# Down projection of a hybrid decoder layer: three of four chunks leave PSUM through ScalarE and reach the residual by accumulating DMAs

## The chip, the cores and the metric

One core of one Trainium2 chip runs the whole program in one launch. The metric is the device time of that core in microseconds (us). Three runs of the kernel before gave a median of 2453.39 us (2452.91 to 2453.67).

## The reference

One layer of a decoder trunk works on 1024 prompt positions and 8 sample positions, which the kernel keeps side by side as 1032 columns. The layer has a recurrent part (two linear recurrences, merged and projected by `w_out`) and then the part that matters here:

```
x  = x + g1 * (u @ w_out)
h2 = rmsnorm(x, norm_mlp) * (1 + sc2) + sh2
x  = x + g2 * (square(relu(h2 @ w_up)) @ w_down)
y  = rmsnorm(x, norm_final)
```

The width is 1024 and the hidden width of the last block is 4096. `g2` is one number for each of the 1024 channels: the same for all prompt positions, another for each of the 8 sample positions. All data are float32.

## The kernel before, in words

Activations are stored transposed: a plane is a tile of 128 channels (the partitions) by `NT` = 1032 columns, so x is eight planes `x1[0]` to `x1[7]`. For float32 accuracy every matmul operand is split into a high part and a remainder, and each product is three matmuls (high by remainder, remainder by high, high by high; lines 89 and 1344). A weight block of 128 by 1024 is loaded by SyncE's queue into a staging tile `wr` (three of them), ScalarE makes the high part `wh` (line 57), VectorE the remainder `wl` (line 58). An activation plane is loaded and split in the same way by `load_split_in` (DMA line 925, ScalarE line 926, VectorE line 927).

The up projection produces 32 hidden planes and stores each to DRAM (`ad[j]`) by DMAs from GpSimd's queue (line 1372). The down projection `x1 += g2 * (hidden @ w_down)` is cut into four chunks c = 0 to 3 of the 4096 hidden channels (loop at line 1429). Each chunk takes eight hidden planes as `X` and has eight output planes m. For chunks 0 to 2, `chunk` (line 977) does:

- m = 0, 1, 2 with `dense` (line 120): three column slices of 344, each 24 matmuls into one PSUM tile of tag `acc` (three of them). Beside them VectorE and ScalarE build the operand sums for what follows (`operand_sums`: loads line 968, differences line 1150, split lines 971 and 972).
- m = 3 and 4, then m = 5 and 6, with `strassen_pair` (line 1317): seven block products p in the order 1, 7, 6, 2, 5, 4, 3, each in two column quarters q of 258, each 12 matmuls. Products 6, 5 and 3 go on accumulating in the bank of product 1, and product 4 in that of product 7. Where a partial sum is also part of another result, `keep` (line 1329) copies it to SBUF by ScalarE (products 1, 6, 7); results come out after products 2, 5, 4 and 3.
- The next chunk's eight planes are loaded and split (`following`), and m = 7 is done with `dense`, whose weight split is cut in two parts.

Chunk 3 does m = 0 to 2 with `dense`, and then, after the loop, m = 3 to 7 by column ranges together with the sum of squares of the final norm, and the store of y.

How a result reaches `x1`: after a dense slice `gated_add` (line 1059) runs one VectorE instruction `x = ps * gate + x` (line 1065); for the columns of the last slice, the 8 sample columns take two more (lines 1068 and 1069). After a pair's product 2, 5 or 4, `add_pair` (line 1417) first adds the kept copy to the PSUM tile on VectorE (line 1423, tile `dt`) and then calls `gated_add`; after product 3 it calls `gated_add` alone.

The order of each engine's instructions is fixed when the program is built: the framework orders them by priority and by its own simulated times, and inserts the waits on tiles, buffers and DMAs. Evacuations are issued at a raised priority (lines 92 and 1348). Each engine then works through its list in order.

Tiles that the change takes up: the tags `mt` (2 buffers), `sq` (2), `nrm_y` (2), `nrm_a`, `nrm_t` and `sqa` (1 each) of 128 by 344 float32, which the up projection and `keep` use.

Of the kernel before, what the change touches and what calls it, by code (L numbers as in the profile page):

```python
# [1 line left out]

# [5 lines left out]
F32 = mybir.dt.float32  # L8
# [3 lines left out]
AF = mybir.ActivationFunctionType  # L12
ALU = mybir.AluOpType
# [4 lines left out]
P = 128  # L18
T = 1024
NB = 8  # L20
NT = T + NB
NS = 3
SW = NT // NS
# [16 lines left out]
def cs(s):  # L40
    return slice(s * SW, (s + 1) * SW)
# [6 lines left out]
def load_w(k, src, prio=AHEAD, tiles=None, parts=1):  # L48

    nc = k.nc  # L50
    with k.tc.high_priority(prio):
        wr = stage(k)[:, :KD * P]
        nc.sync.dma_start(wr, src)
        wh, wl = tiles or [k.wp.tile([P, KD * P], F32R, tag=t, name=t, bufs=2) for t in ("wh", "wl")]
        for n in range(parts):
            c = slice(n * KD * P // parts, (n + 1) * KD * P // parts)
            nc.scalar.activation(wh[:, c], wr[:, c], AF.Copy)  # L57
            nc.vector.tensor_tensor(wl[:, c], wr[:, c], wh[:, c].bitcast(F32), op=ALU.subtract)  # L58
    return wh, wl
# [60 lines left out]
def dense(k, src, X, evac, parts=1):  # L120

    w = load_w(k, src, parts=parts)
    return [dense_split(k, w, X, s, evac) for s in range(NS)]
# [935 lines left out]
def gated_add(k, s, dst, base, ps, gate):  # L1059

    nc = k.nc
    c = cs(s) if isinstance(s, int) else s
    w = c.stop - c.start
    n = w if c.stop < NT else w - NB
    nc.vector.scalar_tensor_tensor(dst[:, :n], ps[:, :n], gate[:, 0:1], base[:, :n], ALU.mult, ALU.add)
    if n < w:
        t = k.sp.tile([P, NB], F32, tag="ga", name="ga", bufs=2)
        nc.vector.tensor_tensor(t, ps[:, n:], gate[:, 1:9], op=ALU.mult)
        nc.vector.tensor_tensor(dst[:, n:], t, base[:, n:], op=ALU.add)
# [60 lines left out]
HQ = NT // 4  # L1130
# [186 lines left out]
def strassen_pair(k, srcs, X, evac, last=3):  # L1317


    nc = k.nc  # L1320
    W = strassen_weights(k, srcs)
    bank = {}
    for n in (1, 2, 3):
        for q in range(2):
            tag, bufs = ("rec", 4) if n == 1 else ("acc", 3) if (n, q) != (3, 1) else ("ada", 1)
            bank[n, q] = k.ps.tile([P, 512], F32, tag=tag, name="b%d" % n, bufs=bufs)[:, :HQ]
    snap = {}

    def keep(p, q, acc):
        pool, tag, bufs = {(1, 0): (k.sp, "nrm_y", 2), (1, 1): (k.sp, "nrm_y", 2), (6, 0): (k.sp, "nrm_a", 1),  # L1330
                           (6, 1): (k.sp, "nrm_t", 1), (7, 0): (k.sp2, "sqa", 1), (7, 1): (k.sp2, "s7", 1)}[p, q]
        t = pool.tile([P, HQ if tag == "s7" else SW], F32, tag=tag, name="s%d" % p, bufs=bufs)[:, :HQ]
        k.kept = nc.scalar.activation(t, acc, AF.Copy)
        snap[p, q] = t

    for p in (1, 7, 6, 2, 5, 4, 3) if last == 3 else (1, 7, 6, 5, 4, 3, 2):
        b = {7: 2, 4: 2, 2: 3}.get(p, 1)
        for q in range(2):
            acc = bank[b, q]
            cols = slice(q * HQ, (q + 1) * HQ)  # L1340
            wh, wl = W[p]
            for i, (xh, xl) in enumerate(X[p]):
                sl = slice(i * P, (i + 1) * P)
                for j, (a, x) in enumerate(((wh, xl), (wl, xh), (wh, xh))):
                    nc.tensor.matmul(acc, a[:, sl], x[:, cols], start=(p in (1, 7, 2) and i == 0 and j == 0),  # L1345
                                     stop=(i == KD // 2 - 1 and j == 2), skip_group_check=True)
                tick(k, 3)
            with k.tc.high_priority(AHEAD):
                if p in (1, 6, 7):
                    keep(p, q, acc)  # L1350
                elif p == 2:
                    evac(0, 0, q, snap[1, q], acc)
                elif p == 5:
                    evac(1, 1, q, snap[7, q], acc)
                elif p == 4:
                    evac(1, 0, q, snap[6, q], acc)
                else:
                    evac(0, 1, q, None, acc)


def phase_ffn(k, x1, h2):
    nc = k.nc
    NF = 4 * KD
    up = k.i["w_up"]
    ad = [k.dp.tile([P, NT], F32, name="ad%d" % j) for j in range(NF)]
    bufs = iter(range(1 << 20))

    def out(j, cols):
        n = next(bufs) % 4
        pool, tag = (k.sp2, "mt") if n < 2 else (k.sp, "sq")  # L1370
        r = pool.tile([P, SW], F32, tag=tag, name="r", bufs=2)[:, :cols.stop - cols.start]
        return r, lambda: nc.gpsimd.dma_start(ad[j][:, cols], r)

    def relu2(r, ps):
        nc.scalar.activation(r, ps, AF.Relu)
        nc.vector.tensor_tensor(r, r, r, op=ALU.mult)

    def evac_up(j):
        def f(s, ps):
            r, store = out(j, cs(s))  # L1380
            relu2(r, ps)
            store()
        return f

    ws = [load_w(k, up[j]) for j in range(2)]
    for j, s in [(j, s) for j in range(2) for s in LAST[:2]] + [(0, LAST[2]), (1, LAST[2])]:
        dense_split(k, ws[j], h2, s, evac_up(j))

    T = {n: [] for n in (1, 2, 3, 4)}
    for j in range(2, 6):  # L1390
        dense(k, up[j], h2, evac_up(j))
        strassen_planes(k, h2, T, j - 2)
    X = strassen_operands(h2, T)
    for n in range(6, NF - 2, 2):
        def evac(m, half, q, a, ps, n=n):
            c = half * HN + q * HQ
            r, store = out(n + m, slice(c, c + HQ))
            if a is None:
                relu2(r, ps)
            else:  # L1400
                nc.vector.tensor_tensor(r, a, ps, op=ALU.add)
                nc.vector.scalar_tensor_tensor(r, r, 0.0, r, ALU.max, ALU.mult)
            store()
        strassen_pair(k, (up[n], up[n + 1]), X, evac)

    def add(m):
        return lambda s, ps: gated_add(k, s, x1[m][:, cs(s)], x1[m][:, cs(s)], ps, k.modT[:, 40 + m, :])

    def act(c, j):
        return load_split_in(k, ad[c * KD + j], half_tag("S0" if c % 2 else "S1", j))  # L1410
    down = k.i["w_down"]
    M0 = 3
    aX = []
    for j in range(NF - 2, NF):
        aX += [act(0, i) for i in range(4 * (j - NF + 2), 4 * (j - NF + 3))]
        dense(k, up[j], h2, evac_up(j))
    def add_pair(m0):
        def evac(m, half, q, a, ps):
            c = half * HN + q * HQ
            c = slice(c, c + HQ)  # L1420
            if a is not None:
                t = k.sp.tile([P, SW], F32, tag="sq", name="dt", bufs=2)[:, :HQ]
                nc.vector.tensor_tensor(t, a, ps, op=ALU.add)
                ps = t
            x = x1[m0 + m][:, c]
            gated_add(k, c, x, x, ps, k.modT[:, 40 + m0 + m, :])
        return evac

    for c in range(4):
        ws = [down[c * KD + m] for m in range(KD)]  # L1430
        if c == 3:
            for m in range(M0):
                dense(k, ws[m], aX, add(m))
            break
        aX = chunk(k, ad[c * KD:(c + 1) * KD], aX, ws, add, add_pair, "S1" if c % 2 else "S0",
                   lambda: [act(c + 1, i) for i in range(KD)])
    free = [k.pp.tile([P, NT], F32R, tag=half_tag("S1", i // 2), name="free") for i in range(16)]
    ws = [load_w(k, down[3 * KD + m], tiles=None if m < M0 + 2 else [free[2 * (m - M0) - 4 + n][:, :KD * P] for n in range(2)])
          for m in range(M0, KD)]
    sq, sq2, sums, ra, rs = [t.bitcast(F32) for t in free[11:]]  # L1440
    for m in range(M0):
        sum_sq(k, sums, x1[m], m == 0, (sq, sq2)[m % 2])
    half = iter(range(1 << 20))
    for c in COLS:
        for m in range(M0, KD):
            x = x1[m][:, c]
            dense_split(k, ws[m - M0], aX, c, lambda s, ps: gated_add(k, s, x, x, ps, k.modT[:, 40 + m, :]))
            o = next(half) % 2 * 512
            sum_sq(k, sums[:, c], x, False, sq[:, o:o + c.stop - c.start])
        y = rstd_model(k, sums[:, c], (ra[:, c], rs[:, c], sums[:, c]))  # L1450
        for m in range(KD):
            x = x1[m][:, c]
            nc.vector.scalar_tensor_tensor(x, x, k.norm_final[:, m:m + 1], y, ALU.mult, ALU.mult)  # L1453
            nc.sync.dma_start(k.o["y"][m][:, c], x)
# [181 lines left out]
```

## Time and profile before

| | |
|---|---|
| median of three runs | 2453.39 us |
| the profiled execution | 2456.04 us |
| its span in the profile | 2454.1 us |
| PE, PEld busy | 2419.3, 2355.8 us |
| DVE, ACT, POOL busy | 1736.0, 1155.7, 112.7 us |
| mean DMA rate | 142 GB/s |

PE is TensorE's matmuls, PEld its weight loads, DVE VectorE, ACT ScalarE, POOL GpSimd, SP SyncE; a q behind a name is that engine's sequencer, which also issues DMAs. A group line names the source line, engine, operation, output and inputs with their shapes, then the count, the busy time in us and the mean in ns, then the idle time ahead of it and what ended it. A line of the windows view gives for a stretch of the span the busy time and the count of each engine, the granted clock of TensorE (PEclk, 1 is full), the mean busy share of the 16 DMA engines and what they moved. The view of one source line gives the shortest, the median and the longest duration of its instructions in ns. Matmuls overlap in a pipeline, so the time of one in a group is longer than the distance from one to the next.

### The profile page before, as it was taken

To read this page: it belongs to the slowest core of one execution; us is meant where nothing else is said; L and a number is where in the kernel's file an instruction comes from. 1 tells how busy PE (TensorE), PEld (TensorE's weight loads), DVE (VectorE), ACT (ScalarE), POOL (GpSimd) and SP (SyncE) were. 2 spreads that over 40 slices of the span, in tenths; PEclk is the share of its full clock that TensorE was granted. 3 is DMA by queue.
4 is the path that set the end of the run, shared out by engine and by line. 5 is a ranking of instruction groups with operands and counts; after the bars stand their busy time and mean duration, and the time that the engine had idled before them with its cause. 6 is when DMAs were issued, how large, how long until landed. Compare 5 with 4: busy or idle time off the path is not lost.

```text
span 2454.1 us, 51952 instructions
## 1 busy us (share of the span) xinstructions
PE 2419.3 (99%) x22014; PEld 2355.8 (96%) x22014; DVE 1736.0 (71%) x3019; ACT 1155.7 (47%) x1859; POOL 112.7 (5%) x218
## 2 busy tenths in 40 slices
PE   8999999999999999999999999999999999999998
PEld 7999999999999999999999899999999999999997
DVE  7656666359888888886687757656976666787755
ACT  4544444366555665534566534533533334343331
POOL 0000000000000000001011000000011222000000
PEclk9999999999999999999999999999999999999999
DMA  7333323334544454535445724634233335354231
GB/s 263 123 112 115 117 100 130 116 93 149 175 136 163 135 179 132 169 146 173 140 158 170 267 91 171 233 130 138 92 109 103 113 110 172 124 190 160 74 130 70
DMA packets 113897, 347.86 MB, mean 142 GB/s; under 512 B 20385, under 2 KB 26385, under 8 KB 113649
## 3 DMA queue, kind: packets, MB, share of 16 engines
q1 hardware_dynamic: 96960, 291.68, 35.0%
q0 software_dynamic: 16272, 52.52, 6.2%
q8 instruction: 172, 2.82, 0.5%
q14 instruction: 61, 0.49, 0.1%
q10 hardware_dynamic: 432, 0.35, 0.0%
HBM read 274.91 MB, written 69.85 MB: 140 GB/s over the span
## 4 chain that ended last, share of the span: by engine, by line
PE 49%; DVE 2%; DMA 2%; ACT 1%; issue 1%; SPq 0%; DVEq 0%; POOL 0%; ACTq 0%; POOLq 0%
PE b L1345 26%; PE acc L90 22%; DMA ybc<-rh 1%; DVE wl L58 0%; DMA lo<-yd 0%; DMA lo<-od 0%; ACT wh L57 0%; PE ss L567 0%; PE ss L1087 0%; DVE lo L927 0%; DVE ht L1116 0%; DVE sqa L1080 0%; DMA lo<-ad 0%; DVE x L1453 0%; DVE h2l L1118 0%
## 5 line engine op out<-in xcount | busy, mean ns | idle before, releaser
L90 PE MATMUL acc<-hl,wh 128*128 128x344 f32 x1608 | 527.6, 328 | 0.1
L90 PE MATMUL acc<-hh,wl 128*128 128x344 f32 x1608 | 516.5, 321 | 0.0
L90 PE MATMUL acc<-hh,wh 128*128 128x344 f32 x1608 | 515.6, 321 | 0.0
L1345 PE MATMUL b<-th,wl 128*128 128x258 f32 x1120 | 317.4, 283 | 0.3
L1345 PE MATMUL b<-tl,wh 128*128 128x258 f32 x1120 | 317.3, 283 | 0.0
L1345 PE MATMUL b<-th,wh 128*128 128x258 f32 x1120 | 315.9, 282 | 0.0
L90 PEld LDWEIGHTS acc<-hl,wh 128*128 128x128 f32 x1608 | 302.3, 188 | 5.2 <-issue 2.8
L90 PEld LDWEIGHTS acc<-hh,wh 128*128 128x128 f32 x1608 | 302.5, 188 | 3.9 <-issue 3.9
L90 PEld LDWEIGHTS acc<-hh,wl 128*128 128x128 f32 x1608 | 302.6, 188 | 0.0
L90 PE MATMUL acc<-lo,wh 128*128 128x344 f32 (+3 forms) x792 | 254.0, 322 | 4.1 <-DVE lo L927 2.5
L90 PE MATMUL acc<-hi,wl 128*128 128x344 f32 (+3 forms) x792 | 254.5, 321 | 0.1
L90 PE MATMUL acc<-hi,wh 128*128 128x344 f32 (+3 forms) x792 | 253.5, 320 | 0.0
L1290 DVE TENSOR_TENSOR wl<-wr,wh 128x512 fp32r<-128x512 f32 (+1 forms) x175 | 157.8, 902 | 97.1 <-ACT wh L1308 53.8
L1345 PEld LDWEIGHTS b<-tl,wh 128*128 128x128 f32 x1120 | 211.5, 189 | 4.5 <-issue 4.5
L57 ACT ACTIVATE wh<-wr 128x1024 fp32r<-128x1024 f32 (+1 forms) x140 | 142.8, 1023 | 152.7 <-PE acc L90 75.4
L1345 PEld LDWEIGHTS b<-th,wl 128*128 128x128 f32 x1120 | 211.6, 189 | 2.7 <-DVE wl L1290 2.7
L1345 PEld LDWEIGHTS b<-th,wh 128*128 128x128 f32 x1120 | 211.4, 189 | 0.0
L58 DVE TENSOR_TENSOR wl<-wr,wh 128x1024 fp32r<-128x1024 f32 (+1 forms) x140 | 165.6, 1184 | 64.6 <-ACT wh L57 63.9
L90 PEld LDWEIGHTS acc<-lo,wh 128*128 128x128 f32 x792 | 149.0, 188 | 6.4 <-DVE lo L927 3.3
L90 PEld LDWEIGHTS acc<-hi,wl 128*128 128x128 f32 x792 | 149.4, 189 | 1.9 <-DVE wl L58 1.0
L90 PEld LDWEIGHTS acc<-hi,wh 128*128 128x128 f32 x792 | 149.4, 189 | 0.8
L756 DVE SCALAR_TENSOR_TENSOR cv<-raw,cst,cv 128x1024 f32<-128x1024 f32 x96 | 122.5, 1276 | 0.5
(342 smaller groups left out, 5219.8 us busy)
## 6 DMA issues: line engine op xcount, KB each, us to landing
wr<-w_ssm SPq DMA_DIRECT2D x48, 512.0 KB
wr<-w_ada SPq DMA_DIRECT2D x36, 512.0 KB
lo<-ad SPq DMA_DIRECT2D x32, 516.0 KB
wr<-w_hg SPq DMA_DIRECT2D x32, 512.0 KB
w<-cumd SPq DMA_DIRECT2D x32, 512.0 KB
wr<-w_up SPq DMA_DIRECT2D x32, 512.0 KB
wr<-w_down SPq DMA_DIRECT2D x32, 512.0 KB
ad<-r POOLq DMA_DIRECT2D x96, 129.0 KB, 2.2
```

The lines of the kernel that those rows point to most:

```text
L57: nc.scalar.activation(wh[:, c], wr[:, c], AF.Copy)
L58: nc.vector.tensor_tensor(wl[:, c], wr[:, c], wh[:, c].bitcast(F32), op=ALU.subtract)
L90: last = nc.tensor.matmul(acc, a[:, sl], b[:, c], start=(i == 0 and j == 0), stop=(i == n - 1 and j == 2))
L756: nc.vector.scalar_tensor_tensor(cv[:, :T], raw[:, j:j + T], cw[:, j:j + 1], cv[:, :T], ALU.mult, ALU.add)
L1290: nc.vector.tensor_tensor(out, x, y, op=ALU.subtract)
L1345: nc.tensor.matmul(acc, a[:, sl], x[:, cols], start=(p in (1, 7, 2) and i == 0 and j == 0), stop=(i == KD // 2 - 1 and j == 2), skip_group ...
```

## The change

Chunks 0 to 2 no longer use `gated_add`. A new function `accumulate` takes one of nine SBUF tiles in turn (the tags above), has ScalarE write `ps * gate` into it (VectorE does the 8 sample columns where there are any), and issues a DMA on GpSimd's queue that adds the tile to `x1[m][:, c]` in SBUF. In the pairs the kept copies are gone: products 1, 6 and 7 are accumulated into the residual themselves, and what came out with a kept copy added now comes out alone. Chunk 3, the up projection and everything before keep their code.

```
+    ring = iter([(k.sp2, "mt", 2), (k.sp, "sq", 2), (k.sp, "nrm_y", 2)] * 2
+                + [(k.sp, "nrm_a", 1), (k.sp, "nrm_t", 1), (k.sp2, "sqa", 1)])
+    ring = itertools.cycle(ring)
+
+    def accumulate(m, c, ps):
+
+        pool, tag, n = next(ring)
+        w = c.stop - c.start
+        r = pool.tile([P, SW], F32, tag=tag, name="r", bufs=n)[:, :w]
+        gate = k.modT[:, 40 + m, :]
+        n = w if c.stop < NT else w - NB
+        nc.scalar.activation(r[:, :n], ps[:, :n], AF.Copy, scale=gate[:, 0:1])
+        if n < w:
+            nc.vector.tensor_tensor(r[:, n:], ps[:, n:], gate[:, 1:9], op=ALU.mult)
+        nc.gpsimd.dma_start(x1[m][:, c], r, accum_op=ALU.add)
...
     def add(m):
-        return lambda s, ps: gated_add(k, s, x1[m][:, cs(s)], x1[m][:, cs(s)], ps, k.modT[:, 40 + m, :])
+        return lambda s, ps: accumulate(m, cs(s), ps)
...
     def add_pair(m0):
         def evac(m, half, q, a, ps):
             c = half * HN + q * HQ
-            c = slice(c, c + HQ)
-            if a is not None:
-                t = k.sp.tile([P, SW], F32, tag="sq", name="dt", bufs=2)[:, :HQ]
-                nc.vector.tensor_tensor(t, a, ps, op=ALU.add)
-                ps = t
-            x = x1[m0 + m][:, c]
-            gated_add(k, c, x, x, ps, k.modT[:, 40 + m0 + m, :])
+            accumulate(m0 + m, slice(c, c + HQ), ps)
+        evac.parts = True
         return evac
```

In `strassen_pair`, after products 1, 6 and 7:

```
-                    keep(p, q, acc)
+                    if hasattr(evac, "parts"):
+                        evac(*{1: (0, 0), 6: (1, 0), 7: (1, 1)}[p], q, None, acc)
+                    else:
+                        keep(p, q, acc)
```

More of the change, by code (lines that the diff above doesn't have):

```diff
@@ L1 @@
+import itertools
 from contextlib import ExitStack
@@ L1349, in strassen_pair @@
                 if p in (1, 6, 7):
-                    keep(p, q, acc)
+                    if hasattr(evac, "parts"):
+                        evac(*{1: (0, 0), 6: (1, 0), 7: (1, 1)}[p], q, None, acc)
+                    else:
+                        keep(p, q, acc)
                 elif p == 2:
-                    evac(0, 0, q, snap[1, q], acc)
+                    evac(0, 0, q, snap.get((1, q)), acc)
                 elif p == 5:
-                    evac(1, 1, q, snap[7, q], acc)
+                    evac(1, 1, q, snap.get((7, q)), acc)
                 elif p == 4:
-                    evac(1, 0, q, snap[6, q], acc)
+                    evac(1, 0, q, snap.get((6, q)), acc)
                 else:
@@ L1432, in phase_ffn @@
             for m in range(M0):
-                dense(k, ws[m], aX, add(m))
+                dense(k, ws[m], aX, lambda s, ps: gated_add(
+                    k, s, x1[m][:, cs(s)], x1[m][:, cs(s)], ps, k.modT[:, 40 + m, :]))
             break
```

## The prediction

> **What bounds the kernel now.** I read the page's busy times first, then the windows of the three chunks that change, then what PE waited for there.
>
> ```profile
> span 2454.1 us, 51952 instructions
> ...
> PE 2419.3 (99%) x22014; PEld 2355.8 (96%) x22014; DVE 1736.0 (71%) x3019; ACT 1155.7 (47%) x1859; POOL 112.7 (5%) x218
> ```
> ```profile
> core 0: us, PE busy (x) PEld busy (x) DVE busy (x) ACT busy (x) POOL busy (x), PEclk, DMA share, GB/s
> 2086.00:2125.10 39.10, 39.10 (x251) 39.10 (x250) 31.60 (x48) 12.22 (x15) 1.63 (x3) 1.00 0.50 167
> 2125.10:2165.75 40.65, 40.63 (x339) 40.35 (x337) 25.76 (x52) 13.72 (x24) 0.00 (x0) 1.00 0.28 93
> 2165.75:2211.16 45.41, 45.41 (x288) 45.31 (x289) 41.01 (x60) 19.14 (x20) 0.00 (x0) 1.00 0.57 197
> 2211.16:2251.90 40.74, 40.71 (x338) 40.43 (x338) 25.79 (x52) 13.91 (x24) 0.00 (x0) 1.00 0.28 93
> 2251.90:2297.28 45.38, 45.38 (x288) 45.38 (x289) 41.24 (x60) 19.06 (x20) 0.00 (x0) 1.00 0.57 198
> 2297.28:2337.90 40.62, 40.56 (x338) 40.28 (x337) 25.80 (x52) 14.08 (x24) 0.00 (x0) 1.00 0.28 93
> ```
> ```profile
> PEld acc L90 <- DVE wl L58: 1.0, 3, 0.4
> ```
> ```profile
> 2125.02 40.40 PE b L1345 x336
> 2165.42 0.31 PE acc L90 x2
> 2165.73 0.02 issue
> 2165.75 45.41 PE acc L90 x286
> ```
>
> The six windows are, in turn, the dense part and the pair part of each chunk (the last m = 7 counts with the next dense part). PE is busy in all 251.9 us but 0.1, at full clock. VectorE is at 41 of 45 us in a dense part, but PE does not wait for it: the whole list of PE's waits over these chunks is three waits of the weight load for the remainder `wl`, 1.0 us together. The chain shows where: each time the pairs end and m = 7 begins, two matmuls take 0.31 us and there is a gap. So VectorE is crowded, and PE sets the time; what the change can save here is that 1.0 us.
>
> **The change, part by part.** These are the rows of what leaves VectorE, over the three chunks:
>
> ```profile
> L1065 DVE SCALAR_TENSOR_TENSOR x<-acc,modT,x 128x344 f32<-128x344 f32 (+1 forms) x36 | 20.4, 568 | 9.3 <-PE acc L90 9.1
> L1065 DVE SCALAR_TENSOR_TENSOR x<-dt,modT,x 128x258 f32<-128x258 f32 (+1 forms) x36 | 17.5, 486 | 1.2
> L1423 DVE TENSOR_TENSOR dt<-s,b 128x258 f32<-128x258 f32 x36 | 15.2, 423 | 21.7 <-PE b L1345 21.7
> L1065 DVE SCALAR_TENSOR_TENSOR x<-b,modT,x 128x258 f32<-128x258 f32 (+1 forms) x12 | 5.7, 474 | 0.0
> L1069 DVE TENSOR_TENSOR x<-ga,x 128x8 f32<-128x8 f32 x23 | 3.7, 161 | 0.3
> L1068 DVE TENSOR_TENSOR ga<-acc,modT 128x8 f32<-128x8 f32 x12 | 1.8, 154 | 0.0
> ```
>
> *VectorE.* 20.4 + 17.5 + 15.2 + 5.7 = 58.8 us, plus 24 pairs of 8-column instructions at 0.154 and 0.161 (7.6 us), go: 66.4 us. Back come 30 multiplications of 8 columns (12 dense slices at the end of a plane, three quarters in each of six pairs) at 0.154: 4.6 us. Net 61.8 us less on an engine that had 191.2 us of work in the six windows. All of it lies beside PE, so it is worth nothing but the three waits.
>
> *ScalarE and GpSimd.* The nearest rows are the up projection's evacuations, the kept copies, and the stores of the same tiles by GpSimd's queue:
>
> ```profile
> L1375 ACT ACTIVATE r<-acc x24: 434/458/461, 1763.0 to 2091.0; 128x344 f32<-128x344 f32 x24
> L1375 ACT ACTIVATE r<-b x24: 367/388/390, 1846.1 to 2070.2; 128x258 f32<-128x258 f32 x24
> ```
> ```profile
> L1333 ACT ACTIVATE s<-b 128x258 f32<-128x258 f32 x36 | 13.7, 383 | 19.3 <-PE b L1345 19.0
> ```
> ```profile
> L1372 POOL DMA_DIRECT2D ad<-r x120: 539/542/547, 1764.3 to 2094.2; - x120
> ...
> DMA to landing us min/median/max: 2.0/2.2/7.1
> ```
>
> 36 dense slices at 0.458 and 84 quarters (14 in each pair) at 0.388 are 16.5 + 32.6 us; the 36 kept copies (13.7 us) go. ScalarE rises by 35.4 us, from 92.1 to 127.5 of 251.9. Behind a waiting evacuation on its list stand the weight and plane splits (lines 57 and 926), and PE waits for those; but PE hands over a quarter every 40.40 / 28 = 1.44 us and a bank of a pair is written again only three quarters later, so an evacuation may be 4 us late. GpSimd gets 120 issues; at 0.542 that is 65 us on an engine that did almost nothing here, and 28 in a pair part are 15.2 of 40.4 us. Only the last three stores of hidden planes are ahead of them.
>
> *The new waits.* A tile of the ring is taken again nine evacuations later, 13.0 us in a pair part; the same columns of x1 are added to again six quarters later, 8.7 us (product 1 then 2, 6 then 4, 7 then 5), and the second DMA must wait for the first. The slowest landing of a plain store was 7.1 us, so both are covered, the second by 1.6 us.
>
> *The DMA engines.* No accumulating DMA is in this trace. A plain copy reads and writes; one that adds also reads its target, three moves for two. I bound its price between the plain row and three times that. The plain price:
>
> ```profile
> DMA packets 10789, 39.47 MB, mean 150 GB/s; under 512 B 1232, under 2 KB 1232, under 8 KB 10768
> q1 hardware_dynamic: 10512, 38.47, 42.5%
> q0 software_dynamic: 256, 0.70, 0.7%
> ...
> ad<-r POOLq DMA_DIRECT2D x3, 172.0 KB, 2.5
> ```
>
> This covers 264 us (2086 to 2350). 39.47 MB took about 43.6% of 16 engines (the two rows and 0.4% of instruction fetch), 115 us, or 0.343 MB per us. A quarter (132 KB) is 0.385 us of all engines, so a pair part's 28 are 10.8 us, and its share rises from 0.28 to about 0.55. That fits. It is tight in one place only, the switch from the pairs to m = 7:
>
> ```profile
> 2156.00:2162.00 6.00, 6.00 (x53) 6.00 (x52) 4.61 (x12) 0.67 (x2) 0.00 (x0) 1.00 0.46 158
> 2162.00:2172.00 10.00, 9.98 (x70) 9.70 (x69) 9.42 (x16) 8.13 (x9) 0.00 (x0) 1.00 1.02 391
> ```
> ```profile
> 2163.07 1.23 DVE L927 TENSOR_TENSOR lo<-lo,hi 128x1032 fp32r<-128x1032 f32 x1
> 2164.22 0.48 DVE L1065 SCALAR_TENSOR_TENSOR x<-dt,modT,x 128x258 f32<-128x258 f32 x1
> 2164.61 0.48 DVE L1065 SCALAR_TENSOR_TENSOR x<-b,modT,x 128x258 f32<-128x258 f32 x1
> 2165.01 0.68 DVE L58 TENSOR_TENSOR wl<-wr,wh 128x512 fp32r<-128x512 f32 x1
> ...
> 2177.09 0.57 DVE L1065 SCALAR_TENSOR_TENSOR x<-acc,modT,x 128x336 f32<-128x336 f32 x1 [0.32 <-PE acc L90]
> ```
> ```profile
> 2161.97 1.07 ACT L926 ACTIVATE hi<-lo 128x1032 fp32r<-128x1032 f32 x1 [4.52 <-PE b L1345]
> 2162.94 1.14 ACT L57 ACTIVATE wh<-wr 128x512 fp32r<-128x512 f32 x2
> ...
> 2174.92 1.07 ACT L926 ACTIVATE hi<-lo 128x1032 fp32r<-128x1032 f32 x1 [0.17 <-DMA lo<-ad]
> ```
> ```profile
> 2158.32 0.33 SPq L925 DMA_DIRECT2D lo<-ad  x1
> ```
>
> VectorE's list here is: remainder of the next chunk's first plane, two residual additions, then the `wl` that PE needs at about 2165.5. Without the two additions `wl` ends 0.8 us earlier, near 2164.9: the gap closes, with 0.6 us to spare. But that first plane must come by DMA, issued at 2158.32 and used at 2161.97, and three accumulations (the second quarter of product 2, both of product 5) now fall in front of it: 1.15 us plain, 1.7 at three moves for two, 3.5 at three times. Less the 0.6 us to spare, PE waits 0.55, 1.1 or 2.9 us. (Product 4's second evacuation, 0.39 us on ScalarE ahead of `wh`, ends before the plane's remainder does and adds nothing.) The last of the eight planes is the second test. Its split starts on ScalarE at 2174.92, so it is ready at 2174.92 + 1.07 + 1.22 = 2177.2; m = 7 ends near 2177.1, and PE comes to the eighth plane after 7 x 3 matmuls at 0.158 (45.41 / 288), at 2180.4: 3.2 us to spare. While the engines are full, about five quarters and one slice (0.84 MB) are added: 2.4 us plain, 3.7 at 1.5 times, 7.3 at three times, so PE waits 0, 0.5 or 4.1 us. The later of the two decides, since a first wait moves the second deadline too.
>
> *The sum.* Three switches, less the 1.0 us that PE waits now: plain 3 x 0.55 - 1.0 = +0.7; 1.5 times 3 x 1.1 - 1.0 = +2.3; three times 3 x 4.1 - 1.0 = +11.3. Better than -1.0 is not to be had, since PE waits for nothing else. At 1.5 times, but with half of the first delay falling into idle engine time (they are 46% busy from 2156 to 2162), the waits are 0.3 and 0.5, and 3 x 0.5 - 1.0 gives +0.5. That and the plain figure lie together; I take +0.6 us, nearest to the plain store's row. The profiled execution took 2456.04 us, of which 2454.1 are the span and 1.9 lie around it; the median of the runs is 2.65 us lower, 0.1%. The same addition on the median gives 2454.0 us.
>
> The plain store's row is the trace's only price for this queue. The Trainium skill's page "Collectives: The Full Stack", under "Part 3: Why 7× under link rate", speaks against the change: a DMA that adds needs two source reads, both go through the reading side's ring, and the rate is half that of a copy. No run here shows it yet. By that rule as an estimate, double price, the sum would be 3 x 1.7 - 1.0 = +4.1 us.
>
> **The rivals.** *Operand loads late at the switch (slower).* The same place as above, with accumulations dear enough to push the plane loads. It decides from a wait of 2.0 us at each switch, which is a last-plane delay of 5.2 us or 2.1 times the plain price; at three times it gives 2464.7 us. For it: the engines are full (1.02) from 2162 to 2172. Against: they are half idle before, and the same tiles landed in 2.2 us in the up projection.
>
> *The queue falls behind the pairs (slower).* If accumulations pass one at a time, s us each, the ring of nine runs out: the 28th evacuation of a pair part needs the 19th DMA done, so the part grows once 19 x s is over 40.4, from s = 2.13 us. At 2.5 us (the landing of the three 172 KB stores in the list above) a pair part loses 7.1 us, 2453.4 + 21.3 = 2474.7 us. Against: 0.542 us to issue, and plain stores overlap their landings.
>
> *An evacuation in front of the weight split.* ScalarE may be given product 3's last quarter ahead of m = 7's `wh`. PE then waits 0.39 + 0.57 + 0.68 = 1.6 us at each switch instead of 0.33: +3.9, 2457.3 us. For it: evacuations have raised priority; against: `wh` has its inputs sooner.
>
> *All of PE's waits go and none comes:* 2452.4 us. For it: VectorE's list is 61.8 us shorter. It is no gain that could be told.
>
> **How the numbers follow.** About 0.2%, 4.9 us, is what a measurement of this kernel can tell from no change: the bounds are 2448.5 and 2458.3. Forecast 0.57, late loads 0.20, queue behind 0.08, evacuation in front 0.10, waits gone 0.05. Slower: 0.18 of the late loads, 0.08, 0.02 of the evacuation order and 0.02 of the forecast's own upper end, 0.30. Faster: 0.03, for a new order of the lists that I can't see. The rest, 0.67, is the same. The range of 2452.0 to 2465.0 takes in late loads up to three times the price and the waits gone, and leaves out the queue behind, dearer loads and a true gain, under 0.2 together.
>
> **What would show it.** Right: PE over 99% busy from 2086 to 2338, VectorE near 129 us and ScalarE near 127 us there, 120 issues on GpSimd near 0.54 us, landings under 8.7 us, and waits at the three switches under 1 us each. Late loads would show as PE waiting for lines 927 or 58 behind a DMA into `lo`; a queue behind as ScalarE's evacuations waiting for a DMA out of `r`, and PE for ScalarE inside the pairs; evacuation in front as line 57 behind a wait for product 3. Wrong: issues over 1.4 us, or landings that grow along a pair part.

## The result and the profile after

The changed kernel took 2469.82 us (median of four runs, 2468.82 to 2470.96) against 2453.15 us for the kernel before on the same chip: a ratio of 1.0069, 95% interval 1.0055 to 1.0084, or 16.7 us more. The forecast was 2454.0 with a range up to 2465.0. Ratios here and below compare fast runs: one run of e2, at 2799 us, was in a slower state of the chip and is left out of its ratio.

The line numbers of the kernel after are one higher than those of before up to 1346 (90 is now 91, 925 to 927 are 926 to 928, 968 is 969); the stores of line 1372 are at 1376 and the evacuations of line 1375 at 1379. New are 1421 (ScalarE's evacuation), 1423 (the 8 columns) and 1424 (the accumulating DMA).

First the page of the kernel after, its span and its busy times:

```profile
span 2467.1 us, 52256 instructions
...
PE 2421.9 (98%) x22014; PEld 2357.6 (96%) x22014; DVE 1685.4 (68%) x2881; ACT 1196.8 (49%) x1943; POOL 218.2 (9%) x338
```

VectorE has lost 50.6 us and the span of this execution is 13.0 us longer than the one profiled before. The windows show where. These are the same pieces as in the prediction, cut where the pairs begin and end, and as a seventh the last switch with all that follows it up to the end of the last dense planes; the columns are those of the prediction's windows (length, busy time of PE, PEld, DVE, ACT, POOL, granted clock, DMA share, GB/s):

```profile
2082.60:2121.70 39.10, 39.10 (x251) 39.10 (x250) 27.04 (x36) 16.17 (x22) 8.67 (x11) 1.00 0.73 198
2121.70:2162.10 40.40, 40.40 (x339) 40.40 (x338) 13.09 (x21) 19.70 (x37) 23.78 (x27) 1.00 0.79 148
2162.10:2212.90 50.80, 47.66 (x291) 46.67 (x290) 36.81 (x44) 26.47 (x35) 11.34 (x13) 0.97 0.87 248
2212.90:2253.30 40.40, 40.40 (x338) 40.40 (x337) 13.09 (x21) 19.92 (x38) 23.70 (x27) 1.00 0.78 150
2253.30:2303.00 49.70, 46.18 (x290) 45.34 (x289) 36.70 (x44) 26.16 (x34) 11.37 (x13) 1.00 0.87 252
2303.00:2343.30 40.30, 40.30 (x338) 40.30 (x338) 13.09 (x21) 19.75 (x38) 23.71 (x27) 1.00 0.80 150
2343.30:2426.60 83.30, 78.50 (x429) 72.67 (x427) 35.83 (x55) 24.48 (x29) 4.36 (x5) 0.96 0.31 95
```

And the kernel before, the three pieces that hold a switch, cut in the same way:

```profile
2165.42:2211.16 45.74, 45.72 (x290) 45.34 (x290) 41.34 (x61) 19.47 (x20) 0.00 (x0) 1.00 0.58 199
2251.56:2297.28 45.72, 45.69 (x290) 45.41 (x290) 41.58 (x61) 19.40 (x20) 0.00 (x0) 1.00 0.57 199
2337.65:2413.59 75.94, 75.87 (x429) 70.10 (x427) 37.02 (x62) 20.81 (x23) 0.00 (x0) 1.00 0.22 78
```

The pair parts and the first dense part are as long as before. The three pieces with a switch grow by 5.06, 3.98 and 7.36 us, 16.4 in all, as much as the medians differ by; the parts of the program that the change doesn't touch were 3.3 us shorter in this execution. PE stands idle in the three for 3.14 + 3.52 + 4.80 = 11.5 us (0.1 before), and is busy 1.94 + 0.49 + 2.63 = 5.1 us longer for the same matmuls (47.66 for 45.72, 46.18 for 45.69, 78.50 for 75.87). What it waited for is in the list of PE's waits of the kernel after from 2064 to 2427 us (releaser, us in total, times, longest):

```profile
PE acc L91 <- DVE lo L928: 10.7, 5, 4.8
PE acc L91 <- DVE r L1423: 0.7, 1, 0.7
```

So the operand planes of the next chunk come late: the prediction's rival of late loads, at all three switches. (The other 0.7 us is a PSUM tile that waits for VectorE's multiplication of 8 columns, at the second switch.) The first of the late planes in order of time, from the timeline of the kernel after:

```profile
2155.42 5.88 SPq L926 DMA_DIRECT2D lo<-ad  x5
2161.59 0.51 SPq L969 DMA_DIRECT2D wr<-ad  x1
2162.14 1.05 SPq L926 DMA_DIRECT2D lo<-ad  x2
...
2174.58 1.06 ACT L927 ACTIVATE hi<-lo 128x1032 fp32r<-128x1032 f32 x1 [2.28 <-DMA lo<-ad]
...
2175.68 1.23 DVE L928 TENSOR_TENSOR lo<-lo,hi 128x1032 fp32r<-128x1032 f32 x1 [1.50 <-ACT hi L927]
...
2176.97 0.43 PE L91 MATMUL acc<-lo,wh 128*128 128x344 f32 x1 [2.58 <-DVE lo L928]
```

The sixth plane loaded is issued at 2162.14, ScalarE can split it only at 2174.58, VectorE ends its remainder at 2176.91, and PE, which had the product before it done 2.58 us earlier, goes on. A load of 516 KB took 12 us. The DMA view says why. For the stretch from the issue of the first plane to the landing of this one (19.2 us, 2155.4 to 2174.6), in the kernel after (queue, packets, MB, share of the 16 engines; then the issues):

```profile
q1 hardware_dynamic: 1305, 4.81, 68.1%
q0 software_dynamic: 1208, 1.10, 38.1%
...
x<-r POOLq DMA_DIRECT2D x7, 129.0 KB, 7.3
x<-r POOLq DMA_DIRECT2D x1, 172.0 KB, 6.8
```

In the kernel before, 2158.4 to 2175.0, while its eight planes come:

```profile
q1 hardware_dynamic: 1463, 5.38, 88.4%
```

SyncE's loads alone filled 88% of all engines there before the change, 1.9 us were free in 16.6. Eight accumulations now bring 38.1% of 19.2 us, 7.3 us of work for all 16 engines. Together the two shares are 106%, and the loads give way: they move 4.81 MB in 19.2 us, where they moved 5.38 MB in 16.6.

The price of an accumulation over the prediction's 264 us (2086 to 2350), in the kernel after:

```profile
q0 software_dynamic: 16735, 17.05, 41.6%
```

17.05 MB held the engines for 41.6% of 264 us, 109.8 us: 0.155 MB per us, where the plain transfers of the kernel before made 0.343. And the two new lines of the program, from the views of lines 1421 and 1424 of the kernel after (shortest, median, longest in ns):

```profile
L1421 ACT ACTIVATE r<-b,modT x84: 449/477/482, 2123.2 to 2346.8; 128x258 f32<-128x258 f32 x66, 128x250 f32<-128x250 f32 x18
L1421 ACT ACTIVATE r<-acc,modT x36: 524/539/552, 2092.6 to 2360.4; 128x344 f32<-128x344 f32 x24, 128x336 f32<-128x336 f32 x12
```
```profile
L1424 POOL DMA_DIRECT2D x<-r x120: 862/872/1245, 2093.5 to 2362.2; - x120
...
DMA to landing us min/median/max: 2.7/5.0/9.2
```

### The profile page after: what moved, and what is told of

The parts are those of the page before. It is cut to its first block, busy times and chain, and to the rows that moved or that the text cites. A ratio compares the mean times of both kernels' runs of the same rounds, so it can differ in the third digit from the quotient of the medians.

```text
span 2467.1 us, 52256 instructions
## 1 busy us (share of the span) xinstructions
PE 2421.9 (98%) x22014; PEld 2357.6 (96%) x22014; DVE 1685.4 (68%) x2881; ACT 1196.8 (49%) x1943; POOL 218.2 (9%) x338
## 3 DMA queue, kind: packets, MB, share of 16 engines
q0 software_dynamic: 33552, 69.96, 10.8%
## 4 chain that ended last, share of the span: by engine, by line
PE 89%; DVE 4%; DMA 3%; ACT 2%; issue 1%; SPq 0%; POOL 0%; DVEq 0%; POOLq 0%; ACTq 0%
PE acc L91 51%; PE b L1346 27%; PE lv_ps L588 2%; DMA lo<-ad 2%; PE y_ps L883 1%; PE kvx_ps L850 1%; PE o_ps L552 1%; PE yi_ps L891 1%; DVE wl L59 1%; PE ada_ps L206 1%; PE kv_ps L535 1%; PE cb_ps L813 1%; PE xt_ps L838 1%; DMA lo<-yd 1%; PE ss L568 0%
```

## The experiments

Four theories stood after the result. A: the accumulations' time on the 16 DMA engines makes the plane loads late. B: the change gave SyncE's queue another order, and the planes stand behind loads that wait for a staging tile. C: ScalarE's longer list holds up the splits. D: the traffic of the whole stage costs, not that near the switch. In the list of SyncE's loads and PE's products at the first switch, B can be seen (from the two programs; numbers are the next chunk's planes, s a load of the operand sums; products of the same plane are for its different column slices):

```
SyncE before  0 4 1 5 6 2 s 7 3 s        PE before  0 1 2 0 1 3 4 5 6 7 2 3 4 ...
SyncE after   0 4 5 1 6 s 2 7 s 3        PE after   0 1 2 0 1 2 0 1 2 3 4 5 6 7 ...
```

**Plain transfers.** e1 is the kernel after with

```
-        nc.gpsimd.dma_start(x1[m][:, c], r, accum_op=ALU.add)
+        nc.gpsimd.dma_start(x1[m][:, c], r)
```

> The 120 DMAs into x1 stay, but as plain copies without the addition (the residual is overwritten, so the addition is left out); the lists of all engines stay as in the changed kernel. Theory A (an accumulating DMA costs the 16 DMA engines 2.2 times a plain one, 41.6% of 264 us for 17.05 MB against 39.7% for 34.97 MB, and so delays the plane loads at the switch): the price falls to 0.385 us a quarter, DMA share of a pair part from 0.79 to about 0.55, PE waits at most 1 us at each switch, 2453 to 2457 us. Theory B (the order of the loads on SyncE's queue changed: a load into a staging tile now stands ahead of the last plane): the order is the same as in the changed kernel, so 2465 to 2470 us.

It took 2458.64 us, ratio 1.0018 (1.0009 to 1.0027). Its waits, and the software queue over the same 264 us:

```profile
PE acc L91 <- DVE lo L928: 4.3, 5, 1.5
```
```profile
q0 software_dynamic: 6449, 17.74, 17.9%
```

About the same bytes hold the engines for 47.3 us instead of 109.8, 0.375 MB per us: an accumulation costs 2.4 times a plain transfer of the same tile. It also takes 2.7 times the packets for its bytes (16735 for 17.05 MB, 6449 for 17.74). Most of the loss is the addition; the transfer itself leaves 4.2 us, which is more than I expected of it.

**Where in the chunk.** e2 accumulates only for m = 0 to 4 and leaves m = 5, 6 and 7 to VectorE as in the kernel before; e3 is the reverse:

```
+        if m < 5:                                   # e3: m >= 5
+            return lambda s, ps: accumulate(m, cs(s), ps)
+        return lambda s, ps: gated_add(k, s, x1[m][:, cs(s)], x1[m][:, cs(s)], ps, k.modT[:, 40 + m, :])
...
+        return evac if m0 < 5 else evac_dve         # e3: m0 >= 5
```

> Accumulating DMAs only for m = 0 to 4 (the dense slices and the first pair, 69 of the 120); m = 5, 6 and 7 by VectorE as before. Theory A, only the transfers close to the switch matter: PE waits at the switches as before, 1 us in all, 2452 to 2455 us. Theory B: the loads on SyncE's queue are back in the old order, also 2452 to 2455. Theory D (what counts is the traffic of the whole stage): 69 of 120 give 0.57 of the loss, near 2463 us.

> Accumulating DMAs only for m = 5, 6 and 7 (51 of the 120), the rest by VectorE as before. Theories A and B: nearly the whole loss, 2465 to 2470 us, with PE's waits only at the three switches, 11 us together. Theory D: 0.43 of the loss, near 2460 us.

e2 took 2454.38 us, 0.9995 (0.9985 to 1.0005), e3 2471.41, 1.0070 (1.0053 to 1.0086). All of the loss lies in m = 5 to 7, and theory D falls. e2 was run once more for its profile:

> The kernel e2 again, for a look: accumulations for m=0 to 4 alone, additions by VectorE for m=5 to 7. The time was 2454.38; the profile should show that accumulations cost as much as in the kernel after (some 0.15 MB/us) while PE's waits at the switches stay near those of the kernel before, 0 to 2 us in all. If the pair parts felt them, PE would be below 99% there.

That run took 2451.10 us and its list of PE's waits from 2060 to 2430 is empty. Its software queue over the 264 us:

```profile
q0 software_dynamic: 10117, 10.79, 25.9%
```

Its accumulations are as dear as the others, 10.79 MB in 68.4 us or 0.158 MB per us. They cost nothing that the time shows, and they fall where nobody is waiting for a load. (SyncE's loads have the order of the kernel before in e2 and that of the kernel after in e3; e4 and e7 below take the order by itself.)

**The lists without the DMAs.** e4 keeps ScalarE's evacuations and lets VectorE add from SBUF:

```
-        nc.gpsimd.dma_start(x1[m][:, c], r, accum_op=ALU.add)
+        nc.vector.tensor_tensor(x1[m][:, c], x1[m][:, c], r, op=ALU.add)
```

> ScalarE scales out of PSUM as in the changed kernel, but VectorE adds the tile to x1 and no DMA is issued. Theory A: 2451 to 2455 us, waits at the switches under 1 us. Theory B (SyncE's queue has the order of the changed kernel) and theory C (ScalarE's longer list delays the splits): 2462 us or more, PE waiting for the remainder of the last plane at each switch.

2454.71 us, 0.9998 (0.9988 to 1.0007). SyncE's list is that of the kernel after, instruction by instruction, and ScalarE's has only some evacuations and two splits of operand sums a few places apart. So B and C cost nothing by themselves that the time shows. PE waits a little for split planes even here (1.6 us, in two waits).

**The price, made of plain transfers.** e6 puts two plain DMAs in place of each accumulation, the second into a tile in DRAM:

```
+    dups = itertools.count()
...
-        nc.gpsimd.dma_start(x1[m][:, c], r, accum_op=ALU.add)
+        nc.gpsimd.dma_start(x1[m][:, c], r)
+        d = k.dp.tile([P, SW], F32, name="dup%d" % next(dups))[:, :w]
+        nc.gpsimd.dma_start(d, r)
```

> After, with each accumulating DMA replaced by two plain ones, one to the residual and one to a DRAM tile of its own (the addition is left out): twice the engine time of one plain DMA, 2 x 17.9% = 36% of the window against 41.6% with accumulation. If the price of an accumulation is the time it holds the 16 DMA engines: most of the loss is there again, 2463 to 2469, PE waits for the split planes (lo L928) of 8 to 11 us. If an accumulation delays in a way of its own (its landing, its issue of 0.87 us): about as with one plain DMA, 2457 to 2461, waits below 6 us.

2472.50 us, 1.0076 (1.0061 to 1.0091); the waits, and the queue over the 264 us:

```profile
PE acc L91 <- DVE lo L928: 10.7, 5, 4.4
PE acc L91 <- DVE r L1424: 0.9, 1, 0.9
```
```profile
q0 software_dynamic: 12261, 33.73, 34.3%
```

With no accumulation at all the same waits are there, to 0.2 us. The time was above what I gave. So the loss needs nothing that only an accumulation does on its way; transfers that fill the engines are enough. The size doesn't follow from the engine time alone: this queue held the engines for 34.3% of the 264 us, less than the accumulations' 41.6%, and lost 17.9 us to their 16.7. Half of its bytes go to DRAM, and why it loses as much with less stays open.

**A late plane with an idle DMA.** In the kernel before, 8 columns of one plane make a round trip through DRAM ahead of its split, at each of the three switches. That is 4 KB each way, 24 KB in all (the expectation below says 32):

```
+    for n in range(trips):
+        tmp = k.dp.tile([P, NB], F32, name="trip%d" % next(TRIPS))
+        nc.gpsimd.dma_start(tmp, raw[:, :NB])
+        nc.gpsimd.dma_start(raw[:, :NB], tmp)
...
+        return load_split_in(k, ad[c * KD + j], half_tag("S0" if c % 2 else "S1", j), trips=1 * (c > 0 and j == 3))
```

> The kernel before, with VectorE's additions, in which at each of the three switches the operand plane i=3 of the next chunk, the last or next to last to be loaded, makes one round trip of 8 columns to DRAM and back on GpSimd's queue ahead of its split: a late operand with almost no traffic (32 KB). If it is the idle PE that costs the clock: PE stands for about 3 to 5 us at each switch (9 to 14 us in all), the rows behind a pause in one piece show a granted clock of 0.5 to 0.9 as in the kernel after, and the time grows by 1.2 to 1.5 times the idle time (11.5 us of idle time went with 16.3 us there): about 2466 to 2473. If the clock fell because of the accumulations' load: the clock stays at 1.00 and the time grows by the idle time alone, as it did with plain DMAs (4.9 us of waits, +4.2 us), 2463 to 2468. The figures of idle time decide, not the time alone.

2470.86 us, 1.0071 (1.0056 to 1.0086). PE's waits, and windows of 4 us in and behind its three pauses of 5.9, 4.6 and 2.4 us (the last window holds the third pause; the one behind it has a clock of 1.00 too):

```profile
PE acc L92 <- DVE lo L933: 12.9, 3, 5.9
```
```profile
2182.00:2186.00 4.00, 2.07 (x7) 2.07 (x8) 3.36 (x4) 1.56 (x2) 0.00 (x0) 0.61 0.40 158
2186.00:2190.00 4.00, 4.00 (x17) 4.00 (x16) 2.29 (x5) 0.00 (x0) 0.00 (x0) 0.54 0.37 133
...
2276.00:2280.00 4.00, 2.55 (x9) 2.56 (x10) 3.84 (x5) 1.30 (x3) 0.00 (x0) 0.50 0.05 19
...
2364.00:2368.00 4.00, 1.65 (x11) 1.36 (x9) 2.54 (x4) 2.02 (x2) 0.45 (x1) 1.00 0.40 102
```

12.9 us of pauses made 16.3 us. After the two long pauses the granted clock (the third figure from the end) is 0.50 to 0.61, with 0.05 to 0.40 of the DMA engines busy; after 2.4 us it stays at 1.00. So it is the idle time of PE that costs the clock, not the traffic. Such rows stand in the kernel after behind its first pause, of 2.58 us:

```profile
2176.00:2180.00 4.00, 2.92 (x13) 2.48 (x13) 3.73 (x6) 3.21 (x5) 0.87 (x1) 0.78 1.04 385
2180.00:2184.00 4.00, 3.55 (x16) 3.28 (x17) 3.97 (x5) 0.35 (x1) 0.87 (x1) 0.79 0.93 205
```

At the second switch, where its 3.5 us of idle time came in three pauses of at most 1.5 us, the clock stayed at 1.00, and PE was busy only 0.5 us longer, against 1.9 and 2.6 at the other two.

**The queue's order together with the accumulations.** e7 is the kernel after with the operand sums' loads held behind all eight planes at the first two switches:

```
+    k.loads = getattr(k, "loads", [])[-7:] + [k.loaded]
...
-        nc.sync.dma_start(r, src[i + 4 * n])
+        d = nc.sync.dma_start(r, src[i + 4 * n])
+        for g in getattr(k, "gate", []):
+            order(k, d, g)
...
+        k.gate = list(k.loads)
```

> After, accumulations as they are, but at the switches 1 and 2 the loads of the next operand sums stand behind all eight plane loads on SyncE's queue (before and after have one or two of them between the planes, and they wait for a staging tile). If the queue standing behind such a load makes about half of the lateness there: PE waits for lo of 3.1 and 3.5 us at these switches fall below 1.5 us each, the third switch keeps its 4.8, time 2460 to 2465. If slow transfers make all of it: waits and time as in the kernel after, 2468 to 2471.

2468.30 us, 1.0061 (1.0044 to 1.0078), not to be told from the kernel after. The waits:

```profile
PE acc L91 <- DVE lo L929: 11.5, 4, 4.9
```

At the first switch PE waited 4.1 us (3.0 in the kernel after), at the second 2.4 (3.5), at the third 4.9 (4.8). My theory that the queue standing behind a staging tile makes half of it falls: with full engines it does not matter much in which order the loads are asked for.

**Which accumulations.** e8 takes m = 7 alone back to VectorE (`if m < 7`, all pairs accumulate), e9 the pair (5,6) alone (`if m < 5 or m == 7`, and `evac if m0 < 5 else evac_dve`):

> After, with VectorE's additions for m=7 alone; m=0 to 6 keep their accumulations. In the kernel after, the eight planes of the first switch are under way from 2155.4 to 2174.6 us, and eight accumulations are issued in that time: seven of 129 KB, of the pair (5,6), and one of 172 KB, of m=7. If it is their engine time in this stretch that makes the planes late (38.1% of 19.2 us = 7.3 us for the eight): the seven of the pair still take about 6.3 us, PE still waits some 7 to 10 us for split planes in all, 2463 to 2469. If it is the dense stretch of m=7 itself, in which the last planes land: little is left, 2454 to 2458.

> The other half: accumulations for m=0 to 4 and m=7, VectorE's additions for the pair (5,6). If the seven accumulations of the pair that lie over the plane loads make the loss: PE's waits for split planes are 0 to 3 us in all, 2453 to 2458. If it is m=7: most of the loss is there, 2462 to 2468.

e8 took 2468.93 us, 1.0061 (1.0046 to 1.0076), e9 2453.81, 1.0000 (0.9990 to 1.0009). PE's waits in e8, then in e9:

```profile
PE acc L91 <- DVE lo L928: 9.7, 5, 3.4
PE acc L91 <- DVE ga L1069: 1.9, 2, 1.5
```
```profile
PE acc L91 <- DVE lo L928: 0.9, 2, 0.6
PE acc L91 <- DVE wl L59: 0.2, 1, 0.2
```

The loss hangs on the accumulations of the pair (5,6), which go out while the planes load. One thing remains mixed: the programs of e9 and e2 have the kernel before's order on SyncE, those of e8 and e3 that of the kernel after. Since e4 has the order of after and loses nothing, and e7 mends it and gains nothing, I take the order for a small part of it; the pair's accumulations under the order of before were not tried.

All but e5 beside each other, with the start of ScalarE's split of the sixth plane loaded at the first switch (always plane 2), counted from PE's first matmul behind the pair (5,6). The waits are those of PE itself; the kernel before has none in its list, its 1.0 us are waits of the weight load. For e2 the waits and the split are those of its second run:

| kernel | time against before, us | PE's waits at the switches, us | plane 2 split from, us |
|---|---|---|---|
| before | 0 | none | 5.0 |
| e9, pair (5,6) by VectorE | -0.6 | 1.1 | 6.1 |
| e2, m = 0 to 4 | 0.0 | none | 6.4 |
| e4, no DMAs | +0.3 | 1.6 | 7.4 |
| e1, plain | +4.2 | 4.9 | 10.2 |
| e7, planes first | +13.7 | 11.5 | 11.6 |
| e6, two plain | +17.9 | 11.6 | 12.0 |
| e8, m = 7 by VectorE | +14.5 | 11.6 | 12.6 |
| after | +16.7 | 11.4 | 12.6 |
| e3, m = 5 to 7 | +17.0 | 10.8 | 13.1 |

PE needs this plane 12.3 us after the pair's end (72 matmuls of m = 7 and six of the planes 0 and 1, at 0.158), and ScalarE and VectorE take another 2.3 us for it. So a split that begins by about 10 us is in time at this switch, and from there the table turns; in e1, at 10.2 us, PE waits 0.2 us for it. Times within about 2.4 us of the kernel before, the half width of the intervals of e2, e4 and e9, can't be told from it. No version beats it: PE stood idle for only 0.1 us in the three pieces, so there was no more than that to win.

## Why the prediction was wrong

*What bounds the kernel, and VectorE's share.* Right: VectorE's relief bought nothing. e4 undoes none of the moved work on ScalarE and keeps a VectorE addition, e9 and e2 take part of it away, and all are at 0.9995 to 1.0000 of the time before. The prediction took the weight load's waits of 1.0 us for time to be won; PE itself was idle for 0.1 us of the 251.9, as the same paragraph says, so that the "- 1.0" of the sum had nothing to take.

*ScalarE and GpSimd.* Too small, without effect. A quarter took 0.477 us and a slice 0.539 where I had 0.388 and 0.458 from evacuations that take no gate. The Trainium skill's page "ScalarE: Activation LUTs", under "What ACT_TABLE_LOAD costs", gives 93 ns more for each operand read from a tile; 0.477 less the kept copies' 0.383 is 0.094, so the trace agrees, and I should have used it. An accumulating issue took 0.872 us and not 0.542; 28 of them are 24 of 40.4 us, still with room. In the six windows ScalarE was at 128 us and VectorE at 140 (forecast 127 and 129). Durations of neighbouring instructions overlap: on VectorE before, 2163.07 + 1.23 ends 0.08 us behind the start of the next, and on ScalarE after, 2162.28 + 1.07 ends 0.09 us behind the next at 2163.26. So sums of rows are more than the busy time: VectorE lost 51 us and not 61.8, and ScalarE's agreement is luck, longer evacuations against overlaps.

*The new waits.* Nearly right: landings went up to 9.2 us, over the 8.7 of the same columns, but only instructions of VectorE and GpSimd waited for that (4.0 and 1.2 us), never PE in a pair part.

*The first test.* PE's wait for the `wl` of m = 7 didn't come: the new list of ScalarE splits that weight at 2159.61, ahead of the first plane (2162.28), and PE's waits name no weight.

*The price of an accumulation: the step that failed.* I bounded it between one and three times the plain row and took a value near plain, since "that and the plain figure lie together". It is 2.2 times that row and 2.4 times the same transfers in e1. The Trainium skill's page "Collectives: The Full Stack" (under "Part 3: Why 7× under link rate") has half the rate for the adding step of a reduce-scatter, because of two source reads; the factor measured here is near it, with a little more on top. No run here shows whether a second read makes the price or the smaller packets (1.0 KB against 2.75 KB on average). But the price alone was not enough: my sum gave +4.1 us at double and +11.3 at three times. Three more terms were short. I let "about five quarters and one slice" fall into the full stretch; it was seven quarters and one slice. I gave the last plane 3.2 us to spare by taking it for the eighth in PE's order, but that order isn't the order of loading: the last plane loaded is plane 3, sixth in PE's list before at the first switch, and plane 2, loaded sixth, is third in both lists. The first plane that came late was plane 2, and the new list of SyncE has a load of the operand sums ahead of it. And I valued a pause at its own length, while the clock added another 5.1 us to 11.5 us of idle time.

*How full the engines were.* The prediction read 1.02 from 2162 to 2172 in the windows and set against it that the engines were 46% busy just before. What counted was the whole stretch of the plane loads, 88.4% busy, 1.9 us free in 16.6.

*The rivals.* The late loads came, beyond their highest price. I set their point of decision at 2.1 times the plain price, about what the price turned out to be, and had the chance at 0.20. The queue did not fall behind the pairs (their windows are 40.3 to 40.4 us), and no evacuation stood in front of the weight split: PE's waits name neither.

## What to carry over

Before work is moved onto DMAs, look at the DMA share in the stretch between the issue and the use of the loads that the next stage needs, not at a mean over the stage; a transfer is free where that has room and pushes the loads where it has none. Count an accumulating DMA of these sizes at 2.4 plain ones until a run of your own says otherwise, and count all that are in flight there. Check a deadline in the order in which PE uses the planes, not in that of the loads. Pauses of PE can be charged again by the clock, here with a quarter (e5) to nearly a half (after) of all pauses on top.

## What the runs showed of the hardware

Accumulating DMAs of 128 x 258 and 128 x 344 float32 from SBUF to SBUF held the engines 2.4 times as long as plain ones (0.155 against 0.375 MB per us), in 2.7 times the packets per byte, and took GpSimd 0.872 us to issue instead of 0.538.

ScalarE's activation of 128 x 258 took 0.094 us more where its scale came from a tile (0.477 against 0.383).

The granted clock falls to a half after a pause, but not at one length. PE's first matmul after a pause, in e6, in e7, and twice in e8:

```profile
2270.03 0.66 PE L91 MATMUL acc<-lo,wh 128*128 128x344 f32 x1 [2.25 <-DVE lo L928]
```
```profile
2270.16 0.43 PE L91 MATMUL acc<-lo,wh 128*128 128x344 f32 x1 [2.44 <-DVE lo L929]
```
```profile
2178.00 0.42 PE L91 MATMUL acc<-lo,wh 128*128 128x344 f32 x1 [2.54 <-DVE lo L928]
...
2273.45 0.65 PE L91 MATMUL acc<-lo,wh 128*128 128x344 f32 x1 [1.08 <-DVE lo L928]
```

After 2.25 us this matmul took 0.66 us and the clock of the window from 2270 to 2272 was 0.50; after 2.44 us it took 0.43 and the clock was 1.00, as after e5's third pause, which was as long. In e8 the clock was 1.00 after 2.54 us, but 0.50 from 2274 to 2278 after a pause of only 1.08 us, the third in 7.3 us (1.42, 1.48 and 1.08, 4.0 in all); three pauses in 7.2 us at the second switch of the kernel after (1.47, 0.65 and 1.40) left it at 1.00. In the kernel after, the clock fell 1.2 us behind the end of the pause of 2.58 us: the matmuls there take 0.32 us from 2177.2 to 2178.0 and 0.49 from 2178.4. The Trainium skill's page "TensorE: Matmul & The Clock Gate", under "Part 1: The HAM clock gate", has only a half and a full clock, set by a free-running window of about 3.4 us, and under "Why this matters for your kernels" it advises against pauses over about 3 us. A free-running window fits pauses of one length that go both ways; the 3 us do not hold here, since 2.25 us in one piece were enough. The 1.00 or 0.50 in windows that fall wholly on one side agree with the two states, and values between are windows that hold both.
